# Keys and queries of both attentions turned into scaled fp16 pairs, keys copied to both row halves by DMA

## The chip, the cores and the metric

The kernel runs on one core of a Trainium2 chip. The metric is the device time of one execution in microseconds (us), lower is better. "PE" is TensorE's matmul side and "PEld" its weight load, "DVE" VectorE, "ACT" ScalarE, "POOL" GpSimd, and "SP" SyncE, whose queue issues most of the DMAs.

## The reference

Two layers of a diffusion trunk over 512 latent tokens (an 8 x 64 grid) and 256 context tokens, width 1024. Each layer has two attentions side by side, both with 8 query heads of 64 channels, and with normalised keys and queries:

```python
hx = _rmsnorm(x, norm_g) * (1.0 + scale_x) + shift_x
px = hx @ w_in
a_k, a_v, b_k, b_v, a_q, b_q, a_z, b_z, g_a, g_b = _split(px, SPLIT_SIZES)
...
qa = _rmsnorm(hs(a_q, NA_HEADS), q_norm_a)
ka = _rmsnorm(hs(a_k, NA_HEADS), k_norm_a)
a_att = _na_latent(qa, ka, va, cka, cva, rpb, rows)    # 8 x 16 window + bias, all context keys
qb = _rope_2d(_rmsnorm(hs(b_q, GQA_Q_HEADS), q_norm_b), pos_row, pos_col)
kb = _rope_2d(_rmsnorm(hs(b_k, GQA_KV_HEADS), k_norm_b), pos_row, pos_col)
b_att = _gqa_latent(qb, k_all, v_all)                  # 2 key/value heads, all 768 keys
out_x = _merge(a_att, b_att, a_z, b_z, g_a, g_b, w_o_a, w_o_b, w_out)
x_new = x + gate_x * out_x
```

In the first layer the context tokens go through the same steps (six blocks of 128 tokens as queries), in the second only the latent ones (four). The q and k norms are vectors of 64 per layer; the score is q·k / 8, to which the neighbourhood attention (NA below) adds a learned bias. The other attention is called GQ.

## The kernel before

Everything is held to fp32 accuracy with products of two-part numbers. A projection splits its weights into hi and lo (`load_w` L397, `load_w2` L412: a DMA into `raw`, the hi cast on ACT, the subtraction on POOL or DVE) and its activations likewise (`hx`), and `mm3` L433 takes three fp32r matmuls per 128 x 128 piece: lines L435, L436 and L437, which make up most of PE's time. `raw` has three buffers, the pair `whi`/`wlo` eight, so a weight load is issued when a cast has freed a buffer.

A layer runs: projection of NA keys (AK), of NA values (AV), of NA queries (AQ), the NA stage head by head, the GQ projections, the GQ stage head by head, and the output projections. The eight weight tiles of a projection are used by all token blocks; in layer 1 the blocks of AV are worked side by side in separate PSUM tiles. Work of the gates and of the z projections (`fill`, matmuls of L435 to L437 into `psf` and `psx`) is spread between the heads' scores, so that PE has something to do while DVE and ACT work on a softmax.

After a projection of keys or queries, each block of 128 tokens is normalised by head (`evac_na` L547, `rope_heads` L578) into a tile `y` (`rr` for GQ) with tokens on the rows. `turn` L524 brings it to channels on the rows: four PE transposes into a PSUM tile, then one ACT operation into the fp32 tile `ka`, `qa`, `kb` or `qb` (L545 with the norm's gain, L543 without). A 128-row piece of it has two heads, one in each half of the rows. `hp["lag"]` says how many blocks a turn runs behind its projection. At the start of a head the pair for the scores is made:

- `stage_k` L869: a DVE cast of 64 x 768 (L872), an ACT cast to the other half of the rows (L873), a DVE subtraction (L874; on POOL for GQ, with a further ACT copy L876).
- `stage_q` L878: an ACT cast (L883) and a DVE subtraction into the other half (L884). `qs` then has q's hi part in one half and its lo part in the other, and a matmul over all 128 rows against `kh`, which has the key in both halves, adds up both products.
- the scores are two fp32r matmuls for each piece, with `kh` and with `kl`: L890 and L891 for GQ and the context, L978 for the NA windows.

Behind the scores come, for NA, one DVE operation that negates the scores, adds the bias and takes the minimum (L981), an exp on ACT (L984), and a normalisation; for GQ, L1161 and L1162 in the same roles, and for the context's own queries L903, L905 and L909. The probabilities become an fp16 pair `h` (L841 on ACT, L842 on POOL or DVE) that SP's DMA transposes (L846) into `ht`, from which the value matmuls (L1002 to L1012, L1178, L1179) read. A head's bias comes by three DMAs (`load_bias` L952) into `bint` and `bedg`. Heads are pipelined: the scores of a head are issued before the values of the head ahead of it.

The program is scheduled: a list scheduler with its own timeline puts the instructions of each engine into an order, so code that is written early can land later. `behind` L473 holds a piece to program order on one engine. On each engine, SP's queue included, instructions run in that order, each waiting for its semaphores.

## Time and profile before

| | |
|---|---|
| median of three runs | 1108.3 us |
| lowest, highest | 1107.35, 1112.0 us |
| the profiled execution | 1111.07 us, span 1109.3 us |
| granted clock of TensorE, mean | 0.991 |
| DVE, ACT, POOL busy | 69%, 56%, 43% of the span |
| DMA, mean | 155 GB/s |

A view by windows gives, for a stretch of the span, the busy time of each engine in it, so a window's width less PE's busy time is PE's idle time there. A view by groups gives for each line and tile how many instructions there were, their summed time, the mean of one in ns, and behind the second bar the idle time just ahead of them with what ended it. In a timeline the columns are start, duration, engine, line and operands; matmuls overlap, so their cadence is read from the starts.

### The profile page before, as it was taken

The page shows a single profiled execution, that of the slowest core. Times are in us where ns is not written, and L with a number is a line of the kernel's source. Part 1 is how long each engine was busy: PE and PEld are TensorE (multiplying, and loading weights), DVE is VectorE, ACT ScalarE, POOL GpSimd, SP SyncE. Part 2 cuts the span into 40 slices and gives each one's busy share as a digit, 9 for nine tenths or more (in the row PEclk, how much of TensorE's full clock was granted, in tenths as well). Part 3 has the DMA queues.
Part 4 walks back from the last instruction along what each step waited for, and adds up shares of the span by engine and source line. Part 5 has one row for each costly group of instructions (what it writes and reads, how often), then busy time and mean ns, then how long its engine had stood idle before and what let it go on. Part 6 is the DMA issues. An engine that isn't in the chain of part 4 may idle for free. (4 is left out here: it accounts for less than half of the span.)

```text
span 1109.3 us, 16937 instructions
## 1 busy us (share of the span) xinstructions
PE 1075.5 (97%) x5672; PEld 879.1 (79%) x5672; DVE 767.4 (69%) x1600; ACT 617.1 (56%) x1236; POOL 473.1 (43%) x397
## 2 busy tenths in 40 slices
PE   8999999999999989989999999999999999999998
PEld 5688888788888868767788878888877888777677
DVE  4667889975377487766777785366997665677473
ACT  6454279776433566765330275444899446786430
POOL 1054235555257154463621354232355472564531
PEclk9999999999999999998999999999999999999999
DMA  9455324554543379789633542453565536879642
GB/s 370 146 171 153 90 68 111 128 138 120 169 131 127 100 184 215 166 228 228 213 101 124 157 147 78 140 163 101 134 149 130 156 107 171 199 229 239 188 152 77
DMA packets 236000, 171.79 MB, mean 155 GB/s; under 512 B 160140, under 2 KB 201864, under 8 KB 234248
## 3 DMA queue, kind: packets, MB, share of 16 engines
q1 hardware_dynamic: 228576, 156.31, 51.6%
q0 software_dynamic: 2368, 7.87, 2.1%
q10 hardware_dynamic: 4968, 6.53, 1.8%
q8 instruction: 45, 0.74, 0.3%
q14 instruction: 43, 0.35, 0.1%
HBM read 115.58 MB, written 17.32 MB: 120 GB/s over the span
## 5 line engine op out<-in xcount | busy, mean ns | idle before, releaser
L842 POOL TENSOR_TENSOR h<-p,h 128x256 f16<-128x256 f32 (+2 forms) x104 | 113.6, 1101 | 160.0 <-ACT h L841 117.7
L422 POOL TENSOR_TENSOR wlo<-raw,whi 128x512 fp32r<-128x512 f32 x70 | 98.0, 1406 | 131.6 <-ACT whi L420 98.7
L435 PE MATMUL psf<-hx,whi 128*128 128x512 f32 (+1 forms) x360 | 138.2, 384 | 2.2 <-DVE zt L627 1.2
L436 PE MATMUL psf<-hx,whi 128*128 128x512 f32 (+1 forms) x360 | 136.1, 378 | 0.0
L437 PE MATMUL psf<-hx,wlo 128*128 128x512 f32 (+1 forms) x360 | 136.1, 378 | 0.0
L435 PE MATMUL psx<-whi,hx 128*128 128x512 f32 (+1 forms) x328 | 121.0, 372 | 0.0
L437 PE MATMUL psx<-whi,hx 128*128 128x512 f32 (+1 forms) x328 | 120.0, 367 | 0.0
L420 ACT CAST whi<-raw 128x512 fp32r<-128x512 f32 x136 | 83.2, 620 | 65.5 <-DMA raw<-in_w_in_dram 46.9
L436 PE MATMUL psx<-wlo,hx 128*128 128x512 f32 (+1 forms) x328 | 119.6, 366 | 0.0
L408 POOL TENSOR_TENSOR wlo<-raw,whi 128x512 fp32r<-128x512 f32 x40 | 59.8, 1499 | 117.7 <-ACT whi L405 74.6
L405 ACT CAST whi<-raw 128x512 fp32r<-128x512 f32 x88 | 54.3, 623 | 96.7 <-PE psx L437 34.2
L508 POOL TENSOR_TENSOR ss<-ss,ehalf 128x8 f32<-128x8 f32 (+2 forms) x40 | 63.6, 1593 | 77.2 <-DVE ss L505 72.2
L841 ACT CAST h<-p 128x256 f16<-128x256 f32 (+2 forms) x136 | 81.7, 616 | 5.3 <-DMA ht<-h 1.3
L422 DVE TENSOR_TENSOR wlo<-raw,whi 128x512 fp32r<-128x512 f32 x66 | 65.3, 992 | 25.9 <-ACT whi L420 24.3
L1161 DVE CUSTOM_DVE_ANT_0 p<-pss,vb 128x768 f32<-128x768 f32 x64 | 60.2, 953 | 31.0 <-PE pss L891 28.9
L1162 ACT ACTIVATE p<-pss,mx 128x768 f32<-128x768 f32 x64 | 57.6, 901 | 41.1 <-DVE mx L1161 40.4
L435 PEld LDWEIGHTS psf<-hx,whi 128*128 128x128 f32 x360 | 68.3, 190 | 14.9 <-ACT zt L625 1.9
L437 PEld LDWEIGHTS psf<-hx,wlo 128*128 128x128 f32 x360 | 68.2, 190 | 12.0
L436 PEld LDWEIGHTS psf<-hx,whi 128*128 128x128 f32 x360 | 68.3, 190 | 10.9
L437 PEld LDWEIGHTS psx<-whi,hx 128*128 128x128 f32 x328 | 61.9, 189 | 10.2
L436 PEld LDWEIGHTS psx<-wlo,hx 128*128 128x128 f32 x328 | 62.0, 189 | 9.5
L435 PEld LDWEIGHTS psx<-whi,hx 128*128 128x128 f32 x328 | 61.8, 189 | 9.1 <-issue 0.2
(338 smaller groups left out, 2984.7 us busy)
## 6 DMA issues: line engine op xcount, KB each, us to landing
raw<-in_w_in_dram SPq DMA_DIRECT2D x168, 256.0 KB, 3.0
rawb<-in_w_ada_dram SPq DMA_DIRECT2D x48, 256.0 KB, 2.8
raw<-in_w_out_dram SPq DMA_DIRECT2D x32, 256.0 KB, 2.9
tg<-gs SPq DMA_DIRECT2D x4, 1536.0 KB, 9.9
rawx<-in_w_ada_dram SPq DMA_DIRECT2D x4, 1024.0 KB, 10.3
rawy<-in_w_ada_dram SPq DMA_DIRECT2D x4, 1024.0 KB, 10.3
gs<-zt ACTq DMA_DIRECT2D x16, 256.0 KB, 2.6
raw<-in_w_o_a_dram SPq DMA_DIRECT2D x16, 256.0 KB, 3.1
```

Of the source, the lines that this page charges most:

```text
L405: S.copy(hi[:, :n], raw[:, :n])
L408: e.tensor_tensor(lo[:, :n], raw[:, :n], F(hi[:, :n]), ALU.subtract)
L420: S.copy(hi, raw)
L422: lo_eng(i).tensor_tensor(lo, raw, F(hi), ALU.subtract)
L435: T.matmul(ps, lhs[0], rhs[0], start=first, stop=False)
L436: T.matmul(ps, lhs[0], rhs[1], start=False, stop=False)
L437: T.matmul(ps, lhs[1], rhs[0], start=False, stop=last)
L508: G.tensor_tensor(ss, ss, ehalf[:, :n], ALU.pow)
L841: S.copy(h[:, 0], p[:, :n])
L842: eng.tensor_tensor(h[:, 1], p[:, :n], h[:, 0], ALU.subtract)
L1161: V.tensor_tensor_reduce(p, pss, lift, -1.0, 3e38, ALU.add, ALU.min, mx[:, 0:1])
L1162: S.activation(p, pss, AF.Exp, bias=mx[:, 0:1], accum_out=r[:, i:i + 1])
```

## The change

`turn` no longer writes fp32. It writes an fp16 pair: hi on ACT, lo as (scaled) source minus hi on DVE, both from the PSUM tile. For keys hi and lo are two tiles of all 128 rows. For queries it works by half of the rows: a head's hi goes to its own half and its lo to the other, so that one 128-row slice is what `qs` was. The blocks 0 and 3 of NA queries, whose tokens are placed in two pieces, take two such sets at half width. `stage_q` and its tiles go; a head uses a slice. `stage_k` becomes two SP DMAs of 64 x 2 x 768 from SBUF to SBUF for an NA head, and two per key head (64 x 1536) for GQ. All score matmuls are fp16.

So that fp16 holds the numbers, the gains are scaled up by 2048 over their largest entry (`head_scales`, `na_scales` and the GQ preparation: a few small DVE operations and a DMA of the norms on ACT's queue), and the scores are scaled back where they are read: a factor in L981, L1161 and the exps. The NA bias has to be scaled the other way: in each layer's AV projection the whole table (1 MB and 0.5 MB) is loaded into `za`, scaled by three ACT operations, and stored to two DRAM tiles, from which `load_bias` reads.

```diff
+    def head_scales(rows, inv, up):
+        S.activation(rows, rows, AF.Abs)
+        V.tensor_reduce(inv, rows, AX, ALU.max)
+        V.tensor_scalar(inv, inv, G_MIN, 1.0 / H_UP, ALU.max, ALU.mult)
+        V.reciprocal(up, inv)
+    def na_scales():
+        t = stp.tile([128, 2, 2, 2], F32, name="nscale")
+        inv, up = t[:, 0], t[:, 1]
+        flat = lambda a: a.rearrange("p l i -> p (l i)")
+        head_scales(nrow, flat(inv), flat(up))
+        V.tensor_tensor(gcol[:, 48:52], gcol[:, 48:52], flat(up), ALU.mult)
+        V.tensor_tensor(na_dq, inv[:, :, 0], inv[:, :, 1], ALU.mult)
+        V.tensor_scalar(na_ndq, na_dq, -1.0, None, ALU.mult)
+        V.tensor_tensor(na_up, up[:, :, 0], up[:, :, 1], ALU.mult)
...
-            src = pt.rearrange("p (j s n) -> p j s n", j=npair, s=2)
-            d = dst[:, :, 0:512].rearrange("p j (s n) -> p j s n", n=64)
-            if t == 0:
-                d = d[:, :, 0:3:2, :]
+            cuts = [(0, 64, 0), (64, 128, 128)] if t == 0 else [(0, 64, 448), (64, 128, 64)]
+        else:
+            cuts = [(0, 128, 128 * t + (64 if perm and t < 4 else 0))]
+        def pair(hi, lo, x, g):
+            if g is None:
+                S.copy(hi, x)
+                V.tensor_tensor(lo, x, hi, ALU.subtract)
             else:
-                src, d = src[:, :, ::-1, :], d[:, :, 1:8:6, :]
-        else:
-            c0 = 128 * t + (64 if perm and t < 4 else 0)
-            src = pt.rearrange("p (j n) -> p j n", j=npair)
-            d = dst[:, :, c0:c0 + 128]
-        if g is None:
-            S.copy(d, src)
-        else:
-            S.activation(d, src, AF.Copy, scale=g)
+                S.activation(hi, x, AF.Copy, scale=g)
+                V.scalar_tensor_tensor(lo, x, g, hi, ALU.mult, ALU.subtract)
+        kind, a, b = dst
+        for n0, n1, c0 in cuts:
+            x = pt.rearrange("p (j n) -> p j n", j=npair)[:, :, n0:n1]
+            da, db = [d[:, :, c0:c0 + n1 - n0] for d in (a, b)]
+            if kind == "k":
+                pair(da, db, x, g)
+                continue
+            for e, d in enumerate((da, db)):
+                own, other = slice(64 * e, 64 * e + 64), slice(64 - 64 * e, 128 - 64 * e)
+                pair(d[own], d[other], x[own], None if g is None else g[own])
...
+        za = big("za")
+        ti, te = za[:, 0:2048].rearrange("p (h n) -> p h n", h=8), za[:, 2048:3072].rearrange("p (h n) -> p h n", h=8)
+        nc.sync.dma_start(ti, bias_int[l].rearrange("h p n -> p h n"))
+        nc.sync.dma_start(te, bias_edge[l].rearrange("h p n -> p h n"))
+        def scale_bias():
+            for c in range(3):
+                c0 = 1024 * c
+                S.activation(za[:, c0:c0 + 1024], za[:, c0:c0 + 1024], AF.Copy, scale=na_up[:, l:l + 1])
+            nc.sync.dma_start(b_int[l].rearrange("h p n -> p h n"), ti)
+            nc.sync.dma_start(b_edge[l].rearrange("h p n -> p h n"), te)
         for t in range(6):
             tok_proj(w, 512, a_hx, t, evac_va)
+            if t == 3:
+                behind(ON_ACT, scale_bias)
             if first:
...
-            def k_tile(e, zero):
-                kh = att["p"].tile([128, 768], F32R, tag=f"kh{e}", name=nm("kh"), bufs=1)
-                kl = att["p"].tile([128, 768], F32R, tag=f"kl{e}", name=nm("kl"), bufs=1)
-                if zero:
-                    V.tensor_scalar(rows(kl, 1 - e).rearrange("p (a b) -> p a b", b=128),
-                                    rows(ident, 1 - e).unsqueeze(1).to_broadcast([64, 6, 128]),
-                                    0.0, None, ALU.mult)
-                return kh, kl
-            def stage_k(src, e, kh, kl, dup):
-                k = rows(src, e)
-                V.tensor_copy(rows(kh, e), k)
-                S.copy(rows(kh, 1 - e), k)
-                (G if dup else V).tensor_tensor(rows(kl, e), k, F(rows(kh, e)), ALU.subtract)
-                if dup:
-                    S.copy(rows(kl, 1 - e), F(rows(kl, e)))
-            def stage_q(src, e):
-                n = 768 if first else 512
-                qs = att["p"].tile([128, n], F32R, tag=f"qs{e}", name=nm("qs"), bufs=1)
-                q = rows(src, e)[:, :n]
-                S.copy(rows(qs, e), q)
-                V.tensor_tensor(rows(qs, 1 - e), q, F(rows(qs, e)), ALU.subtract)
-                return qs
+            def stage_k(src, j, e, to):
+                for half in range(2):
+                    nc.sync.dma_start(rows(to, half), rows(src, e)[:, :, j, :])
+            def q_pair(src, e, j):
+                return src[:, e, j, :]
...
-                if late:
-                    V.tensor_scalar(mx, mx, P_LOG, None, ALU.add)
+                dq = gq_dq if late else na_dq[:, l:l + 1]
+                V.tensor_scalar(mx, mx, dq, P_LOG if late else 0.0, ALU.mult, ALU.add)
                 p = p_tile()
                 r = sp.tile([128, 2], F32, tag="r", name=nm("r"), bufs=8)
                 for i in range(2):
                     S.activation(p[:, 256 * i:256 * i + 256], pss[:, 256 * i:256 * i + 256], AF.Exp,
-                                 bias=mx[:, i:i + 1], accum_out=r[:, i:i + 1])
+                                 bias=mx[:, i:i + 1], scale=dq, accum_out=r[:, i:i + 1])
                 if not late:
                     softmax_tail(p, 512, r, mx, [(0, 256), (256, 512)])
...
-                nc.sync.dma_start(bint[:, 0:256], bias_int[l, h])
+                nc.sync.dma_start(bint[:, 0:256], b_int[l][h])
                 for i in range(2):
                     nc.sync.dma_start(bedg[64 * i:64 * i + 64, 128 * i:128 * i + 128],
-                                        bias_edge[l, h, 64 * i:64 * i + 64])
+                                        b_edge[l][h, 64 * i:64 * i + 64])
             turns = big("ht").bitcast(F16)
...
+                    V.tensor_tensor_reduce(p[:, :512], pss, bedg if i == 0 else bint, na_ndq[:, l:l + 1], 3e38,
                                            ALU.add, ALU.min, mx[:, 0:1])
                     r = sp.tile([128, 2], F32, tag="r", name=nm("r"), bufs=8)
...
-            akt = [k_tile(e, True) for e in range(2)]
+            akt = [att["p"].tile([128, 2, 768], F16, name=nm("kk"), bufs=1) for _ in range(2)]
             def na_first(h):
                 j, e = h // 2, h % 2
-                kh, kl = akt[e]
-                stage_k(kav[:, j, :], e, kh, kl, False)
-                q = stage_q(qav[:, j, :], e)
+                kh, kl = akt[e][:, 0], akt[e][:, 1]
+                stage_k(kav, j, e, akt[e])
+                q = q_pair(qav, e, j)
                 st = na_scores(h, q, kh, kl)
                 if not first:
...
-            V.tensor_scalar(gbc[:, 1, :], gbc[:, 1, :], 8.0, None, ALU.mult)
+            vbig = big("vb")
+            g_inv, g_up = vbig[:, 2952:2954], vbig[:, 2954:2956]
+            gq_dq, gq_ndq = vbig[:, 2956:2957], vbig[:, 2957:2958]
+            g_abs = vbig[:, 1920:2048].rearrange("p (a d) -> p a d", a=2)
+            S.copy(g_abs, gbc)
+            head_scales(g_abs, g_inv, g_up)
+            V.tensor_scalar(gbc[:, 0, :], gbc[:, 0, :], g_up[:, 0:1], None, ALU.mult)
+            V.tensor_scalar(gbc[:, 1, :], gbc[:, 1, :], g_up[:, 1:2], 8.0, ALU.mult, ALU.mult)
+            V.tensor_tensor(gq_dq, g_inv[:, 0:1], g_inv[:, 1:2], ALU.mult)
+            V.tensor_scalar(gq_ndq, gq_dq, -1.0, None, ALU.mult)
+            V.tensor_scalar(vbig[:, 2950:2951], g_up[:, 0:1], g_up[:, 1:2], -P_LOG, ALU.mult, ALU.mult)
             def make_tabs(i):
...
+            kbv = hp["p"].tile([128, 2, 1, 768], F16, name=nm("kb"), bufs=1)
+            kb_to = ("k", kbv[:, 0], kbv[:, 1])
+            gkt = big("gk").bitcast(F16)[:, 0:3072].rearrange("p (e x n) -> p e x n", e=2, x=2)
             def evac_bkv(t, ps):
                 rs = head_rstd(ps[:, 0:128], 2)
...
-                    stage_k(kbv[:, 0, :], e, gkt[e][0], gkt[e][1], True)
+                    stage_k(kbv, 0, e, gkt[:, e])
...
-                    V.tensor_tensor_reduce(p, pss, lift, -1.0, 3e38, ALU.add, ALU.min, mx[:, 0:1])
-                    S.activation(p, pss, AF.Exp, bias=mx[:, 0:1], accum_out=r[:, i:i + 1])
+                    V.tensor_tensor_reduce(p, pss, lift, gq_ndq, 3e38, ALU.add, ALU.min, mx[:, 0:1])
+                    S.activation(p, pss, AF.Exp, bias=mx[:, 0:1], scale=gq_dq, accum_out=r[:, i:i + 1])
                     turned(p, 768, ht[:, i], G if i in SPLIT_POOL else V)
```

Three places in the engines' queues. First SP at the AV projection of layer 1; `raw` are tiles of AV's weights, `cb` and `rawb` belong to the modulation. Before:

```order
L403 DMA raw_7300<-in_w_in_dram 128x512
L286 DMA cb_7282<-cd 128x512
L290 DMA rawb_7448<-in_w_ada_dram 128x512
L290 DMA rawb_7451<-in_w_ada_dram 128x512
L403 DMA raw_7306<-in_w_in_dram 128x512
L403 DMA raw_7312<-in_w_in_dram 128x512
L403 DMA raw_7318<-in_w_in_dram 128x512
```

and with the change:

```order
L428 DMA raw_7334<-in_w_in_dram 128x512
L311 DMA cb_7316<-cd 128x512
L315 DMA rawb_7490<-in_w_ada_dram 128x512
L315 DMA rawb_7493<-in_w_ada_dram 128x512
L428 DMA raw_7340<-in_w_in_dram 128x512
L798 DMA za_7370<-in_bias_int_dram 128x8x256
L799 DMA za_7370<-in_bias_edge_dram 128x8x128
L428 DMA raw_7346<-in_w_in_dram 128x512
```

The two loads of the bias table stand between the fourth (`raw_7340`) and the fifth (`raw_7346`) of AV's eight weight tiles.

Second, PE with the change, where the fifth of these tiles is first used (`whi_7348` is the cast of `raw_7346`; `whi_7324`, `whi_7330`, `whi_7336` are of the first three; `psx_7373`, `psx_7401`, `psf_7429`, `psx_7457` are four token blocks of AV). The first matmul of AV is 44 rows ahead of the row with `whi_7348`:

```order
L462 MATMUL psx_7457<-whi_7324,hx_6712 128x512
L460 MATMUL psx_7457<-whi_7330,hx_6710 128x512
L461 MATMUL psx_7457<-wlo_7332,hx_6710 128x512
L462 MATMUL psx_7457<-whi_7330,hx_6712 128x512
L460 MATMUL psx_7373<-whi_7348,hx_6711 128x512
L460 MATMUL psx_7401<-whi_7348,hx_6711 128x512
```

The four blocks run side by side through the first four weight tiles; before, a block was mostly finished ahead of the next.

Third, SP in the NA stage of layer 1, for about one head. Before:

```order
L846 DMA_TRANSPOSE ht_1571_7883<-h_1581_7912 128x4x64 x2
L846 DMA_TRANSPOSE ht_1571_7883<-h_1586_7928 128x4x128
L846 DMA_TRANSPOSE ht_1571_7883<-h_1591_7943 128x4x128
L953 DMA bint_1569_7877<-in_bias_int_dram 128x256
L955 DMA bedg_1570_7878<-in_bias_edge_dram 64x128 x2
L629 DMA zs_79<-zt_1708_8460 128x512
L846 DMA_TRANSPOSE ht_1571_7883<-h_1596_7958 128x4x128
```

and with the change:

```order
L910 DMA kk_1554_7947<-ka_1373_7046 64x2x768 x2
L893 DMA_TRANSPOSE ht_1553_7946<-h_1560_7967 128x4x64 x2
L893 DMA_TRANSPOSE ht_1553_7946<-h_1565_7983 128x4x128
L893 DMA_TRANSPOSE ht_1553_7946<-h_1570_7998 128x4x128
L893 DMA_TRANSPOSE ht_1553_7946<-h_1575_8013 128x4x128
L981 DMA bint_1551_7940<-b_int1_84 128x256
```

The copies of a coming head's keys (`kk`) stand ahead of the transposes of the present head. They wait until PE has issued the last score that reads the same `kk` tile, two heads back.

More of the change, by code (lines that the diff above doesn't have):

```diff
@@ L35 @@
 P_UP = 2.0 ** 14
+H_UP = 2.0 ** 11
+G_MIN = 1.0e-6
 SPLIT_POOL = (1, 3)
@@ L130, in hybrid_kernel @@
     cd = drp.tile([16, 128], F32, name="cd")
+    b_int = [drp.tile([8, 128, 256], F32, name=f"b_int{i}") for i in range(2)]
+    b_edge = [drp.tile([8, 128, 128], F32, name=f"b_edge{i}") for i in range(2)]
     gs = [drp.tile([128, 4, NTOK], F32, name=f"gs{c}") for c in range(4)]
@@ L779, in layer @@
         for t in range(qt):
-            tok_proj(w, 512, a_hx, t, evac_na(qav, True, gq, YB if first else 4))
+            tok_proj(w, 512, a_hx, t, evac_na(("q", qav[:, 0], qav[:, 1]), True, gq, YB if first else 4))
             if t == 0:
@@ L980, in na_scores @@
                     mx = sp.tile([128, 2], F32, tag="mx", name=nm("mx"), bufs=8)
-                    V.tensor_tensor_reduce(p[:, :512], pss, bedg if i == 0 else bint, -1.0, 3e38,
+                    V.tensor_tensor_reduce(p[:, :512], pss, bedg if i == 0 else bint, na_ndq[:, l:l + 1], 3e38,
                                            ALU.add, ALU.min, mx[:, 0:1])
@@ L1479, in _layout @@
                                 + [d['b_ada'][:, 2048:].reshape(16, 128)])
-    d['gvec'] = np.concatenate([d[n][l] for l in range(2) for n in ('q_norm_b', 'k_norm_b')])[None]
+    d['gvec'] = np.concatenate([d[n + b][l] for b in 'ba' for l in range(2) for n in ('q_norm_', 'k_norm_')])[None]
     qc, qr = np.arange(128) // 8, np.arange(128) % 8
```

37 lines of the change are left out of this document (19 added, 18 removed).

## The prediction

> **What bounds the kernel now.** I read the page's busy times first, then PE's idle time by windows, then what PE waited for.
>
> ```profile
> PE 1075.5 (97%) x5672; PEld 879.1 (79%) x5672; DVE 767.4 (69%) x1600; ACT 617.1 (56%) x1236; POOL 473.1 (43%) x397
> 92.00:145.00 53.00, 53.00 (x262) 43.73 (x261) 42.20 (x98) 20.31 (x33) 17.45 (x10) 1.00 0.39 113
> 145.00:250.00 105.00, 101.69 (x616) 86.86 (x615) 94.47 (x250) 86.14 (x193) 52.41 (x56) 1.00 0.48 117
> 380.00:460.00 80.00, 73.59 (x409) 60.33 (x408) 61.60 (x111) 52.59 (x103) 38.17 (x26) 0.96 0.77 181
> 460.00:530.00 70.00, 65.13 (x355) 51.91 (x353) 45.34 (x82) 44.99 (x85) 35.90 (x26) 0.95 0.88 224
> 782.40:862.10 79.70, 78.08 (x416) 62.01 (x416) 70.91 (x197) 72.44 (x160) 40.58 (x45) 1.00 0.59 138
> 410.00:420.00 10.00, 8.47 (x27) 6.67 (x28) 8.85 (x19) 5.50 (x12) 3.70 (x4) 0.66 0.70 165
> 500.00:510.00 10.00, 9.78 (x44) 8.84 (x45) 4.38 (x11) 5.62 (x11) 4.57 (x4) 0.68 1.16 245
> ```
>
> The columns are the window, its width, busy times of PE, PEld, DVE, ACT and POOL with counts, the granted clock, the DMA share and GB/s. PE is busy 1075.5 of 1109.3 us, so 33.8 us are idle in all. Work taken from DVE or ACT is worth at most what it takes out of these 33.8 us; work taken from PE counts nearly in full. A third of the idle time, 6.41 + 4.87 = 11.3 us, lies in the GQ stage of layer 0 (380 to 530). There the clock also fell twice: 8.47 x 0.34 = 2.9 us and 9.78 x 0.32 = 3.1 us of PE time were lost to it. So 17.3 us are lost in that stage. In the NA stages (145 to 250, and 782 to 862 in layer 1) PE idles 3.3 and 1.6 us. In 92 to 145, where keys and queries of layer 0 are projected, it never idles.
>
> ```profile
> PE pss L890 <- ACT p L1162: 4.3, 3, 2.7
> PE pst L853 <- DVE mx L905: 2.9, 1, 2.9
> 406.77 4.61 DVE L297 CUSTOM_DVE_ANT_0 rawb<-rawb,vb 128x512 f32<-128x512 f32 x1
> 493.94 3.60 DVE L842 TENSOR_TENSOR h<-p,h 128x768 f16<-128x768 f32 x1 [0.32 <-ACT h L841]
> 489.54 7.18 POOL L672 TENSOR_TENSOR gal<-za,gah 128x768 fp32r<-128x768 f32 x4
> ```
>
> These are PE's two largest waits and what lies behind them. The DVE operations at 406.77 and 493.94 were held for 4.61 and 3.60 us. The second ends, at 497.5, just after POOL's four back-to-back operations (489.54 + 7.18 = 496.7). L905 and L1162 of the waits stood behind them. The change removes neither of these DVE operations.
>
> **PE's own gain.** Score matmuls go from fp32r to fp16. Their counts, one of each pair:
>
> ```profile
> L890 PE MATMUL pss<-gk,qs 128*128 128x512 f32 x64 | 28.5, 445 | 5.6 <-ACT p L1162 4.3 <-ACT p L909 1.3
> L890 PE MATMUL pss<-gk,qs 128*128 128x256 f32 x80 | 23.1, 292 | 0.0
> L978 PE MATMUL pss<-kh,qs 128*128 128x512 f32 x48 | 19.2, 400 | 0.0
> L890 PE MATMUL pss<-kh,qs 128*128 128x384 f32 x16 | 6.3, 391 | 0.0
> 938.23 0.39 PE L890 MATMUL pss<-gk,qs 128*128 128x512 f32 x1
> 938.46 0.40 PE L891 MATMUL pss<-gk,qs 128*128 128x512 f32 x1
> 938.70 0.28 PE L890 MATMUL pss<-gk,qs 128*128 128x256 f32 x1
> 946.96 0.38 PE L1179 MATMUL pst<-ht,vb 128*128 128x512 f16 x1
> 947.18 0.38 PE L1178 MATMUL pst<-ht,vb 128*128 128x512 f16 x1
> 947.39 0.38 PE L1179 MATMUL pst<-ht,vb 128*128 128x512 f16 x1
> ```
>
> Twice 64 x 512, 80 x 256, 48 x 512 and 16 x 384, with 16 x 128 and 16 x 256 beside the latter in NA, are 180,224 columns, or 352 times 512. The fp32r starts are (938.70 - 938.23) / 2 = 0.235 us apart, the fp16 starts (947.39 - 946.96) / 2 = 0.215. That is 352 x 0.019 = 6.6 us; I take **-6.4**, since pieces of 128 columns can hardly gain. The other end is 0, if the weight loads of short pieces stood in the way.
>
> ```profile
> L891 PEld LDWEIGHTS pss<-gk,qs 128*128 128x128 f32 x144 | 28.0, 194 | 4.3
> L1178 PEld LDWEIGHTS <-vb 128*128 128x128 f16 x96 | 9.4, 98 | 12.1 <-issue 2.6 <-DMA raw<-in_w_o_a_dram 0.3
> ```
>
> But the load shrinks from 194 to 98 ns, below the 108 ns of a 256-column piece, so I stay near -6.4.
>
> **Work moved on DVE and ACT.**
>
> ```profile
> L872 DVE CAST kh<-ka 64x768 fp32r<-64x768 f32 x16 | 10.0, 625 | 2.3 <-PE pst L529 1.4 <-PE pss L978 0.7
> L874 DVE TENSOR_TENSOR kl<-ka,kh 64x768 fp32r<-64x768 f32 x16 | 16.6, 1038 | 0.3
> L884 DVE TENSOR_TENSOR qs<-qb,qs 64x768 fp32r<-64x768 f32 x8 | 9.3, 1159 | 2.4 <-ACT qs L883 2.2
> L884 DVE TENSOR_TENSOR qs<-qa,qs 64x768 fp32r<-64x768 f32 x8 | 8.8, 1099 | 0.2
> L873 ACT CAST kh<-ka 64x768 fp32r<-64x768 f32 x16 | 13.3, 833 | 1.3 <-PE pss L890 0.7 <-PE pss L978 0.3
> L832 DVE SCALAR_TENSOR_TENSOR ho<-psv,vsa,ho 64x512 f32<-64x512 f32 x14 | 10.5, 749 | 12.4 <-ACT ho L831 11.6 <-POOL h L842 0.7
> L545 ACT ACTIVATE qa<-pst,gcol 128x512 f32<-128x512 f32 x10 | 6.7, 684 | 3.6 <-PE pst L529 3.6
> ```
>
> An NA head of layer 0 loses 0.63 + 1.04 + 1.10 = 2.8 us on DVE and 0.83 on ACT, and its q cast besides. A GQ head there loses 1.16 us on DVE. Added is, at the turns, one DVE operation like L832's (a product and a difference out of PSUM) for each block of keys and two for each of queries, 0.75 us each, and a second ACT operation of 0.68 for queries. For the six query blocks of layer 0 these are 9.0 us on DVE. They fall into 92 to 145, where DVE has 42.2 of 53: it then has about 51, still covered by PE's full 53 us, and the first heads' staging no longer follows. Should DVE be late there, the transposes of `y` are late next, by up to the 9.0 us less the 2.8 us of each of the first two heads, 3.4. I take **+1** (0 to +4).
>
> In the NA stages DVE and ACT have less to do by 3 us a head; PE idles there 4.9 us in all. I take **-2** (0 to -4.9). In the GQ stage of layer 0 the relief is 8 x 1.16 = 9.3 of DVE's 107 us, a twelfth, and about as much of ACT's. Since the held operations remain but the order around them is new, I take somewhat under a third of the 17.3: **-5** (0 to -17.3; a new collision as long as the old ones would be +6: a wait of 2.9 and 3.1 of clock).
>
> The small operations of the scales, the norm's DMA and one more DVE operation for each context score lie beside PE's full stretches: **+0.5** (0 to +2; a start-up stall has no other work to hide it).
>
> **The bias table ahead of AV's weights in layer 1.** 1.5 MB are loaded by SP right ahead of the fifth weight tile.
>
> ```profile
> tg<-gs SPq DMA_DIRECT2D x4, 1536.0 KB, 9.9
> DMA to landing us min/median/max: 10.2/10.2/10.2
> 686.60 19.04 SPq L403 DMA_DIRECT2D raw<-in_w_in_dram  x13
> 686.41 0.62 ACT L405 CAST whi<-raw 128x512 fp32r<-128x512 f32 x1
> 690.04 0.62 PE L435 MATMUL psx<-whi,hx 128*128 128x512 f32 x2
> ```
>
> A load of this size took 9.9 us, and a 256 KB weight tile issued right behind such loads, at 489.20, landed after 10.2 us (the second row, that tile alone). The fourth weight tile of AV is issued at 686.60, the table at about 687.1 and 687.6, the fifth tile at 688.1; it lands at 698.3, and with a cast of 0.62 and a subtraction of 1.5 it is ready at 700.4. PE begins AV at about 690.3, and the new order puts 43 matmuls of 0.23 us and a set of transposes (0.6) ahead of the first use: 700.8. That is met by 0.4 us; **+1** (0 to +8: a landing 5 us later, and 3 us at the low clock). The stores and the table of layer 0 have over ten microseconds to spare on both sides of their places.
>
> [...]
>
> **The key copies on SP.**
>
> ```profile
> L846 SPq DMA_TRANSPOSE ht<-h x40: 1169/1218/1981, 782.4 to 860.8; - x40
> L953 SPq DMA_DIRECT2D bint<-in_bias_int_dram x16: 340/532/1134, 136.1 to 844.4; - x16
> L955 SPq DMA_DIRECT2D bedg<-in_bias_edge_dram x32: 472/550/993, 138.1 to 840.3; - x32
> ```
>
> Forty transposes in 78.4 us are eight heads of 10.0 us in layer 1. Of these SP spends 5 x 1.22 + 0.53 + 2 x 0.55 = 7.7 us on the head itself and some 1.5 us on weights and stores that it issues in between: 9.2 of 10.0. Two copies of the kind of L955 (64 rows) add 1.1: 10.3. So SP becomes as full as PE in this stage. A head's order may still shift load into the neighbouring stretches, which is why I take **+2.5** and not 8 x 0.3 with queueing on top (0 to +11, below). In layer 0 a head has more blocks and SP has room. The GQ copies have tens of microseconds until the first score.
>
> **Sum:** -6.4 + 1 - 2 - 5 + 0.5 + 1 + 2.5 = -8.4. The profiled execution took 1111.07, 2.8 above the median of the three runs; from its own time the sum gives 1102.7, from the median 1099.9. Later times stand beside the median, so I forecast **1100**.
>
> **Rivals.** (A) The two collisions and low clocks in the GQ stage vanish altogether: -17.3 in place of -5 and -4.9 in place of -2, so 1085 at best, and 1092 with half of that. For it speaks that DVE and ACT are both lighter, against it that L297, L842 and L672 stay. Chance 0.13.
>
> (B) The gain is returned: fp16 scores only make PE wait for the softmax, which is no shorter, or the weight loads take the 6.4 back. Then what remains is -7 + 1 + 0.5 + 1 + 2.5 = -2, **1106**. For it speaks that L890 waited for ACT's exp; against it that most stretches have no idle time at all. Chance 0.20.
>
> (C) SP becomes the bound of the NA stage in layer 1. If each head waits 1 us more in the queue (a transpose blocked behind a copy that waits for PE's last score of two heads back), a head takes 11.4 and not 10.0: 8 x 1.4 = 11 in place of 2.5, and the gains of the NA and GQ stages are not there: -6.4 + 1 + 0.5 + 1 + 11 = +7, **1115**. What is queued behind a copy is the transposes, for which PE's values wait, and behind these the next scores. It decides from the point where SP's work for a head passes PE's. For it speaks the 9.2 of 10.0; against it that a copy's turn comes once the scores it waits for are issued. Chance 0.22.
>
> **Numbers.** The forecast has 0.45. A measurement of this kernel tells about 0.5%, 5.5 us, from no change: faster is below 1102.8, slower above 1113.8. The forecast's own range, from the neighbouring values of its terms, is 1093 to 1107; 1102.8 cuts it at two thirds, so 0.32 of it is faster and 0.13 the same. A is all faster. Of B 0.03 is faster, 0.15 the same and 0.02 slower, of C 0.02 the same and 0.20 slower. That gives 0.48, 0.30 and 0.22. The losing ends of several terms (+4, +8, +6) can come together and go beyond C, so 0.05 moves from the same to slower. The range of 8 in 10 runs from 1089 (between A's half and its best) to 1118, a little beyond C.
>
> **What would show it.** Score starts 0.215 us apart, and PE's busy time down by about 6 us; L872 to L884 gone and DVE busy by some 20 us less; the first fifth-tile matmul of AV in layer 1 waiting for at most 1 us; PE's waits for `ht` in the NA stage of layer 1 below 3 us. Wrong would be a longer cadence with the separate weight loads, PE idle above 6 us in that NA stage with SP's queue without a gap, or new waits for DVE in 92 to 145.

## The result and the profile after

The changed kernel takes 1138.95 us (median of 5 runs, 1136.84 to 1141.91) against 1109.04 for the kernel before (5 runs): a ratio of 1.027, 95% interval 1.024 to 1.030. It is 30 us slower where 8 us less were forecast. Sixteen further versions were run to find out which part of the change costs what; the fastest of them stands at 0.997 of the kernel before.

The busy times on the page of the changed kernel's profiled execution (span 1140.0 us):

```profile
PE 1080.4 (95%) x5672; PEld 849.9 (75%) x5672; DVE 756.2 (66%) x1627; ACT 608.6 (53%) x1219; POOL 451.1 (40%) x393
```

PE's idle time goes from 33.8 to 1140.0 - 1080.4 = 59.6 us. DVE and ACT both have less to do, by 11 and 9 us, so the change did lighten them, but the time is longer all the same. PE's busy time rises by 5 us although its score matmuls are shorter (381 ns for 512 columns in NA, where they took 397 to 400); more of it runs at the low clock (mean granted clock 0.983 against 0.991).

To see where the time went, both programs are cut at the same events: the first and last score of each NA stage, the first DVE scan of each GQ stage, its last value matmul. The widths, read from the starts of these instructions:

| stage (us) | before | after | difference |
|---|---|---|---|
| start to first NA score, layer 0 | 151.5 | 156.2 | +4.7 |
| NA stage of layer 0 | 115.8 | 114.5 | -1.3 |
| GQ projections of layer 0 | 109.4 | 109.9 | +0.5 |
| GQ stage of layer 0 | 161.3 | 161.2 | -0.1 |
| to the first NA score of layer 1 | 238.2 | 244.7 | +6.5 |
| NA stage and GQ projections of layer 1 | 148.5 | 165.1 | +16.6 |
| GQ stage of layer 1 | 119.6 | 121.0 | +1.4 |
| rest | 65.0 | 67.4 | +2.4 |

The NA stage of layer 1 and the projections behind it are taken together, since the schedule moves `fill` matmuls between them. Windows of both, before first, then after (width, busy times of PE, PEld, DVE, ACT, POOL with counts, clock, DMA share, GB/s):

```profile
776.20:924.70 148.50, 146.31 (x799) 120.46 (x799) 115.47 (x284) 106.54 (x231) 77.35 (x75) 1.00 0.52 136
```

```profile
786.50:951.60 165.10, 149.02 (x798) 115.23 (x796) 108.87 (x281) 97.94 (x218) 72.22 (x73) 0.98 0.53 137
```

The same number of matmuls, 799 and 798, takes 16.6 us longer: PE idles 16.1 us in place of 2.2, and the clock drops to 0.98. DVE, ACT and POOL have less to do, and the DMA engines move 137 GB/s against 136. SP's queue is not in these rows. Its timeline in the changed kernel, and PE's behind it:

```profile
847.04 1.13 SPq L983 DMA_DIRECT2D bedg<-b_edge  x2
848.27 14.02 SPq L893 DMA_TRANSPOSE ht<-h  x10
862.34 0.57 SPq L662 DMA_DIRECT2D gs<-zt  x1
863.01 0.94 SPq L442 DMA_DIRECT2D raw<-in_w_in_dram  x2
864.04 1.20 SPq L893 DMA_TRANSPOSE ht<-h  x1
```

```profile
866.93 0.79 PE L460 MATMUL psx<-hx,whi 128*128 128x512 f32 x1 [6.15 <-ACT whi L445]
867.52 0.63 PE L461 MATMUL psx<-hx,whi 128*128 128x512 f32 x1
867.95 0.63 PE L460 MATMUL psf<-hx,whi 128*128 128x512 f32 x1
868.38 0.63 PE L461 MATMUL psf<-hx,whi 128*128 128x512 f32 x1
```

Ten transposes in a row keep SP for 14 us; the weight tiles for PE's filling work stand behind them and are issued at 863.0, cast at 866.3, and PE has waited 6.15 us. After that its starts are 0.43 us apart and not 0.23, at a granted clock of 0.50 from 866.9 to 872.0. The wait is named after ACT's cast (L445), but ACT itself had sat idle for 1.03 us until the DMA of that tile landed, and the DMA had its turn in the queue only at 863.0.

PE's largest waits over the whole run show the other losers:

```profile
PE psf L460 <- DVE tg L740: 9.0, 6, 3.6
PE psx L460 <- ACT whi L445: 6.6, 2, 6.1
PE pss L918 <- ACT p L1199: 6.5, 3, 3.5
PE psv L1030 <- DVE ho L879: 3.7, 2, 2.3
```

`L1199` is the exp of GQ and `tg` a DVE operation of the output gates that shares DVE with GQ's scans. Two rows of the groups show what became of the operations in these chains:

```profile
L1198 DVE CUSTOM_DVE_ANT_0 p<-pss,vb 128x768 f32<-128x768 f32 x64 | 64.1, 1013 | 28.7 <-PE pss L919 23.9 <-POOL h L889 4.3
L1199 ACT ACTIVATE p<-pss,mx,vb 128x768 f32<-128x768 f32 x64 | 63.5, 993 | 46.8 <-DVE mx L1198 44.2 <-PE psv L900 2.4
```

and the same of the kernel before, with the exp of the context's scores:

```profile
L1161 DVE CUSTOM_DVE_ANT_0 p<-pss,vb 128x768 f32<-128x768 f32 x64 | 60.2, 953 | 31.0 <-PE pss L891 28.9 <-POOL h L842 1.5
L1162 ACT ACTIVATE p<-pss,mx 128x768 f32<-128x768 f32 x64 | 57.6, 901 | 41.1 <-DVE mx L1161 40.4 <-ACT zt L625 0.4
L909 ACT ACTIVATE p<-pss,mx 128x256 f32<-128x256 f32 x32 | 14.9, 469 | 10.3 <-DVE mx L905 6.4 <-DVE h L842 3.6 <-DVE mx L903 0.2
```

The scan took 953 ns and the exp 901; now 1013 and 993. The shape is the same; what is new is that the factor is read from memory (`vb` among the exp's inputs) where it was a constant of the instruction.

### The profile page after: what moved, and what is told of

Same layout as the page of the kernel before. It is cut to its first block, busy times and chain, and to the rows that moved or that the text cites. A ratio compares the mean times of both kernels' runs of the same rounds, so it can differ in the third digit from the quotient of the medians.

```text
span 1140.0 us, 16941 instructions
## 1 busy us (share of the span) xinstructions
PE 1080.4 (95%) x5672; PEld 849.9 (75%) x5672; DVE 756.2 (66%) x1627; ACT 608.6 (53%) x1219; POOL 451.1 (40%) x393
## 5 line engine op out<-in xcount | busy, mean ns | idle before, releaser
L889 POOL TENSOR_TENSOR h<-p,h 128x256 f16<-128x256 f32 (+2 forms) x104 | 108.5, 1051 | 166.0 <-ACT h L888 127.9
L460 PE MATMUL psf<-hx,whi 128*128 128x512 f32 (+1 forms) x360 | 140.6, 391 | 4.4 <-ACT zt L658 2.2
L461 PE MATMUL psf<-hx,whi 128*128 128x512 f32 (+1 forms) x360 | 137.7, 383 | 0.0
L445 ACT CAST whi<-raw 128x512 fp32r<-128x512 f32 x136 | 83.1, 621 | 79.2 <-DMA raw<-in_w_in_dram 48.7
L460 PE MATMUL psx<-whi,hx 128*128 128x512 f32 (+1 forms) x328 | 121.0, 371 | 0.0
L447 DVE TENSOR_TENSOR wlo<-raw,whi 128x512 fp32r<-128x512 f32 x66 | 70.0, 1063 | 42.2 <-ACT whi L445 41.0
L1199 ACT ACTIVATE p<-pss,mx,vb 128x768 f32<-128x768 f32 x64 | 63.5, 993 | 46.8 <-DVE mx L1198 44.2
L1198 DVE CUSTOM_DVE_ANT_0 p<-pss,vb 128x768 f32<-128x768 f32 x64 | 64.1, 1013 | 28.7 <-PE pss L919 23.9
L460 PE MATMUL psx<-hx,whi 128*128 128x256 f32 (+1 forms) x208 | 70.5, 339 | 6.6 <-ACT whi L445 6.6
L462 PE MATMUL psx<-hx,wlo 128*128 128x256 f32 (+1 forms) x208 | 69.8, 335 | 0.2 <-POOL wlo L447 0.2
## 6 DMA issues: line engine op xcount, KB each, us to landing
rawy<-in_w_ada_dram SPq DMA_DIRECT2D x4, 1024.0 KB, 11.1
```

Source lines behind the costliest of these rows:

```text
L445: S.copy(hi, raw)
L447: lo_eng(i).tensor_tensor(lo, raw, F(hi), ALU.subtract)
L460: T.matmul(ps, lhs[0], rhs[0], start=first, stop=False)
L461: T.matmul(ps, lhs[0], rhs[1], start=False, stop=False)
L462: T.matmul(ps, lhs[1], rhs[0], start=False, stop=last)
L889: eng.tensor_tensor(h[:, 1], p[:, :n], h[:, 0], ALU.subtract)
```

## The experiments

Two kinds of runs. The first take one part out of the changed kernel; the second put one part alone into the kernel before. All are compared with runs of the kernel before on the same chip (1108.6 to 1109.3). Each edit goes through the scheduler again, so the order of other instructions can change with it.

### Parts taken out of the change

**Key copies of NA from ACT's queue** (in `stage_k`; `late` is true for NA heads):

```diff
-                    nc.sync.dma_start(rows(to, half), rows(src, e)[:, :, j, :])
+                    (S if late else nc.sync).dma_start(rows(to, half), rows(src, e)[:, :, j, :])
```

> The key copies of the NA heads are issued by ACT's queue instead of SP's; nothing else differs from the changed kernel (1139 us). Theory Q (SP's queue is full in the NA stage of layer 1, and weight tiles and transposes wait behind its other work): the stage and the GQ projections behind it, 165 us from first score to first GQ score in the changed kernel against 148.5 before, shrink to 150 to 155, and the time to 1122 to 1130. Theory D (it is the DMA traffic or the landing of the copies themselves that costs): within 3 us of 1139. Theory S (the softmax chains are longer, because exp and the DVE scan take their factor from memory): within 3 us of 1139 too.

1131.8 us (ratio 1.021, 1.020 to 1.023): 7 us are gone, and the stage and projections of layer 1 take 159.3 us, not the expected 150 to 155. So SP's queue matters. What the rest is, the copies themselves or their waits in ACT's order, this run does not tell.

**Key copies by engines** (the DMAs stay for GQ):

```diff
+                if late:
+                    V.tensor_copy(rows(to, e), rows(src, e)[:, :, j, :])
+                    S.copy(rows(to, 1 - e), rows(src, e)[:, :, j, :])
+                    return
                 for half in range(2):
                     nc.sync.dma_start(rows(to, half), rows(src, e)[:, :, j, :])
```

> The NA keys are put into both halves by one DVE copy and one ACT copy of 64 x 2 x 768 fp16 for each head, with no DMA. Theory Q: as with ACT's queue or better, 1120 to 1130, less what the copies cost on engines that are about 70% busy there. Theory D: the same gain, since the traffic goes too, so this run beats the one with ACT's queue by more than 5 us only if D holds. Theory S: within 4 us of 1139.

1122.7 us (1.013, 1.011 to 1.016), 16 us below the changed kernel; the two stages take 151.7. It beats the run from ACT's queue by 9 us, which by what was expected speaks for the copies' traffic as well. In the kernel before, the runs below rule the traffic out; from ACT's queue the copies cost 2.9 us there, and what the other 6 us of this difference are stays open.

**No bias table:** the loads, the scaling and the stores go, and the heads read the unscaled table, so the scaling of the NA bias is left out.

> The bias table is neither loaded into za, scaled nor stored; the heads read the unscaled table, so the scaling of the NA bias is left out. Theory Q: the AV stage of layer 1 showed no wait of PE for weights, and the table's loads and stores lie elsewhere in SP's queue than the NA stage, so 1134 to 1140. Rival B (the table's 6 MB of transfers and six ACT operations hold up the start of both layers, 3.3 and 2.9 us, and what follows): 1128 to 1134.

1129.6 us (1.019, 1.017 to 1.021), 9 us less. The start is 2.3 us shorter, the NA stage of layer 0 by 4.5, and the two stages of layer 1 by 6.4.

**Constant factors** in the exps, scans and context maxima (one constant for all; the true scales are left out):

```diff
-                    V.tensor_tensor_reduce(p, pss, lift, gq_ndq, 3e38, ALU.add, ALU.min, mx[:, 0:1])
-                    S.activation(p, pss, AF.Exp, bias=mx[:, 0:1], scale=gq_dq, accum_out=r[:, i:i + 1])
+                    V.tensor_tensor_reduce(p, pss, lift, -2.0e-5, 3e38, ALU.add, ALU.min, mx[:, 0:1])
+                    S.activation(p, pss, AF.Exp, bias=mx[:, 0:1], scale=2.0e-5, accum_out=r[:, i:i + 1])
```

> The factors in the exps, the DVE scans and the context maxima are constants of the program (2.0e-5 for all), not values read from memory; the true scales are left out. Theory S: DVE's L1198 falls from 1013 to about 955 ns and ACT's exp from 993 to about 900 ns, the GQ stages (161.2 and 121.0 us) shrink by 3 to 5 us each, and the time goes to 1128 to 1134. Theory Q: the durations may fall but the time stays within 4 us of 1139, since PE waits in the NA stage of layer 1 for other things.

1128.1 us (1.018, 1.016 to 1.019). The exp is back at 900 ns and the scan at 953 (means), and the GQ stage of layer 0 shrinks from 161.2 to 149.7, with 13 matmuls fewer in it and a granted clock of 1.00 against 0.95; that of layer 1 does not shrink (123.9, with 10 more matmuls in it).

With 16 us for the copies, these gains come to 36 us, more than the loss of 30. Each run is also a new schedule, and two runs that take several parts out at once show that the gains do not add.

**No scales at all** (plain values in the fp16 pairs; neither table nor factors nor the operations for them), key copies on SP:

> The changed kernel with no scaling anywhere: no factors from memory, no bias table through za, no small operations for the scales; the fp16 pairs hold the plain values. Key copies stay on SP. If the three costs add up (table -9.5 by the run without it, constant factors -11 by the run with constants, both from 1139), 1116 to 1122, with the key copies' 8 to 16 us left in the NA stage of layer 1 (at least 160 us from its first score to the first GQ score, 148.5 before). If the order of the schedule decides and not these costs, anything between 1110 and 1135, with the gain in other stages than those of the two single runs (start -2.3, GQ stage of layer 0 -11.5).

1133.3 us (1.022, 1.019 to 1.025): above the expected 1116 to 1122. The start (152.6) and the GQ stage of layer 0 (150.6) have their gains, but the two stages of layer 1 take 164.1 us, as in the changed kernel. So the gain of the table and the factors did not reach these two stages; the next run shows that the copies on SP stand in its way.

**No scales, key copies by engines:**

> The same with the NA keys put into both halves by one DVE and one ACT copy for each head. Theory Q (SP's queue costs the rest): 8 to 16 us below the run before, 1102 to 1110, that is, about the kernel before the change or under it; the NA stage of layer 1 and the GQ projections take 146 to 152 us. If Q was the only cause and the scales only an order's luck, it is the same as the run with engine copies and scales, 1120 to 1125.

1112.7 us (1.004, 1.003 to 1.006), above the expected 1102 to 1110. Now the two stages take 149.6. Copies on SP or on engines are worth 20.7 us here.

### Parts put into the kernel before

**The copies alone.** Two SP DMAs of the changed kernel's bytes for each NA head, into a tile that nobody reads:

```diff
                 stage_k(kav[:, j, :], e, kh, kl, False)
+                for half in range(2):
+                    nc.sync.dma_start(dum[64 * half:64 * half + 64, :], F(kh)[64 * e:64 * e + 64, :])
```

> The kernel before the change, with two more SP copies of 64 x 768 fp32 (192 KB, the bytes of the changed kernel's copies) from SBUF to SBUF for each NA head, into a tile that nobody reads. Theory Q: SP is busy 9.2 of 10.0 us for a head of layer 1, and these take it over that: the NA stage of layer 1 and the GQ projections go from 148.5 to 155 us or more, the time to 1114 to 1126; layer 0, where SP has room, stays within 2 us. Rival T (the copies only hurt because the new kernel's turns and heads are ordered otherwise): 1106 to 1112.

1125.5 us (1.015, 1.012 to 1.018): +16.7 from 32 DMAs that the kernel does not need. The two stages of layer 1:

```profile
773.10:937.70 164.60, 151.56 (x799) 121.32 (x799) 119.40 (x285) 107.48 (x231) 80.20 (x75) 0.98 0.52 137
```

164.6 us for 799 matmuls, where the kernel before took 148.5; the NA stage of layer 0 is unchanged (115.6). PE idles 13.0 us there in place of 2.2 and is busy 5.3 us longer, at a granted clock of 0.98. That the width falls within half a microsecond of the changed kernel's 165.1 is in part luck, since PE's waits are others: the longest is 3.8 us ahead of a value matmul (`psv`, L1002), where the changed kernel's 6.15 us stood ahead of the filling work.

**The same DMAs with next to no bytes,** 64 x 16 in place of 64 x 768 (`dum[..., 0:16]`):

> The kernel before with two more SP copies for each NA head, as in the run with full copies (1125.5 us, stage and GQ projections of layer 1 164.6 instead of 148.5), but of 64 x 16 fp32, 4 KB. Theory Q (what costs is SP's issue time and the waits in its order): 1118 to 1126, the two stages 158 us or more. Theory D (it is the 384 KB a head that the DMA engines carry beside transposes and weights): 1107 to 1113.

1124.7 us (1.014, 1.012 to 1.016), and in the two stages:

```profile
773.90:938.20 164.30, 151.28 (x800) 120.90 (x800) 120.58 (x285) 107.49 (x231) 79.08 (x75) 0.98 0.45 123
```

A fiftieth of the bytes, 4 KB for 192, and the loss is the same. Traffic is ruled out: what costs is that SP issues two more DMAs a head. Their issue times on SP's queue (minimum, median and maximum in ns), with the full bytes, in this run, and of the changed kernel's copies:

```profile
L1044 SPq DMA_DIRECT2D dum<-kh x32: 461/498/1296, 147.4 to 847.8; - x32
```

```profile
L1044 SPq DMA_DIRECT2D dum<-kh x32: 461/500/1032, 146.5 to 848.2; - x32
```

```profile
L910 SPq DMA_DIRECT2D kk<-ka x32: 607/644/1689, 144.7 to 866.6; - x32
```

A rival would be that a copy holds the queue while it waits for its own data or its tile. The traces speak against it. In the changed kernel, between the first and the last transpose of layer 1's NA heads, no pause of SP over 0.11 us stands ahead of a copy; with the full dummy copies there is none over 0.05 from 815 to 850, and with the tiny ones no wait of 0.8 us or more ahead of a copy from 776 to 870. Why two short issues a head are too many is seen in SP's timeline of the kernel before. These five rows have its two longest pauses, 0.69 us ahead of 813.35 and 1.44 ahead of 815.13:

```profile
811.67 0.51 SPq L629 DMA_DIRECT2D zs<-zt  x1
812.29 0.37 SPq L417 DMA_DIRECT2D raw<-in_w_in_dram  x1
813.35 0.34 SPq L953 DMA_DIRECT2D bint<-in_bias_int_dram  x1
815.13 1.16 SPq L955 DMA_DIRECT2D bedg<-in_bias_edge_dram  x2
816.51 7.02 SPq L846 DMA_TRANSPOSE ht<-h  x5
```

From 782.4 to 862.0, the 79.6 us in which the forty transposes are issued, all pauses over 0.3 us come to about 3 us. Otherwise one issue follows the other within 0.3 us, mostly 0.05 to 0.1, and this step between two issues takes queue time too. So the queue had about 0.4 us a head to spare. Two issues of 0.50 us with their steps are about 1.2 us a head, 0.8 more than was free: some 6 us for eight heads, an estimate. PE's longer busy time at the low clock (5.3 us with the full copies) comes on top; the remaining 5 us or so are not split.

**The full copies from ACT's queue:**

```diff
-                    nc.sync.dma_start(dum[64 * half:64 * half + 64, :], F(kh)[64 * e:64 * e + 64, :])
+                    S.dma_start(dum[64 * half:64 * half + 64, :], F(kh)[64 * e:64 * e + 64, :])
```

> The kernel before with the full copies of 192 KB, issued by ACT's queue instead of SP's. Theory Q: most of the 17 us goes, 1108 to 1114; what is left is ACT's issue time. Theory D: 1120 to 1127, as from SP.

1112.2 us (1.003, 1.001 to 1.004), the two stages 153.4. So most of the 16.7 us belongs to SP's queue and not to the copies.

**The factors alone,** 1.0 and -1.0 read from memory:

```diff
-                    S.activation(p, pss, AF.Exp, bias=mx[:, 0:1], accum_out=r[:, i:i + 1])
+                    S.activation(p, pss, AF.Exp, bias=mx[:, 0:1], scale=na_dq[:, l:l + 1], accum_out=r[:, i:i + 1])
```

> The kernel before with the factors of the exps, of the DVE scans and of the context maxima read from memory (1.0 and -1.0), so its results do not change. Theory S: DVE's scan goes from 955 to about 1013 ns, ACT's exp from 902 to about 993, and the time to 1112 to 1120, the excess in the two GQ stages. If S is wrong and the runs with constants owe their gain to another order: 1107 to 1111.

1118.9 us (1.008, 1.005 to 1.011), +9.7. The groups of this run:

```profile
L1163 DVE CUSTOM_DVE_ANT_0 p<-pss,vb,ehalf 128x768 f32<-128x768 f32 x64 | 64.4, 1013 | 30.5 <-PE pss L894 28.2 <-POOL h L845 1.4 <-issue 0.4
L1164 ACT ACTIVATE p<-pss,mx,ehalf 128x768 f32<-128x768 f32 x64 | 63.4, 991 | 49.1 <-DVE mx L1163 48.8
L911 ACT ACTIVATE p<-pss,mx,ehalf 128x256 f32<-128x256 f32 x32 | 17.8, 560 | 14.1 <-DVE mx L907 9.3 <-DVE h L845 3.3 <-DVE r L798 1.3
```

+60 ns for a scan and +90 for an exp, at both lengths of the exp: the context's, of 256 columns, goes from 469 to 560. The stages of GQ are wider by 1.4 and 5.6 us, the two stages of layer 1 by 2.5; the new schedule moved `fill` matmuls between stages, so the excess can't be split more finely.

**The table alone,** with a factor of 1.0:

> The kernel before with the round trip of the bias table (loads into za, three ACT operations with a factor of 1.0, stores, heads read the copy). Theory B (the table costs by itself, up to the 9.5 us by which the run without it was faster): 1112 to 1118, of which some 2 us before the first score of layer 0. Rival: it is covered, 1107 to 1111.

1110.8 us (1.001, 1.000 to 1.003): +1.6, covered. So most of the 9 us that its removal gave belonged to the new schedule or to the state of SP's queue, not to the table's transfers; which of the two, no run tells.

**fp16 score operands alone,** same staging operations as before:

```diff
-                kh = att["p"].tile([128, 768], F32R, tag=f"kh{e}", name=nm("kh"), bufs=1)
+                kh = att["p"].tile([128, 768], F16, tag=f"kh{e}", name=nm("kh"), bufs=1)
```

and so for `kl`, `qs` and `gk`.

> The kernel before the change, with only the type of the scores' operands changed: kh, kl and qs are fp16 tiles, filled by the same ACT, DVE and POOL operations as before. The term of -6.4 us says 1100 to 1104, with PE's score starts 0.215 us apart and PE busy some 6 us less. Rival B (the gain is returned as waits or lost to weight loads): 1106 to 1110.

1106.2 us (0.9985, 0.997 to 1.000). Page and timeline of this run:

```profile
PE 1068.6 (97%) x5672; PEld 844.4 (76%) x5672; DVE 759.2 (69%) x1600; ACT 615.5 (56%) x1236; POOL 472.1 (43%) x397
...
935.50 0.39 PE L890 MATMUL pss<-gk,qs 128*128 128x512 f16 x1
935.72 0.38 PE L891 MATMUL pss<-gk,qs 128*128 128x512 f16 x1
935.94 0.27 PE L890 MATMUL pss<-gk,qs 128*128 128x256 f16 x1
936.05 0.27 PE L891 MATMUL pss<-gk,qs 128*128 128x256 f16 x1
```

PE's busy time falls by 6.9 us and the starts are 0.22 and 0.11 us apart, as reckoned. But only 2.6 us reach the end. PE idles 2.1 us more in the GQ stage of layer 0, 2.0 more in that of layer 1, and 2.6 in the two stages of layer 1.

### Relief for SP

The last four runs move the three bias DMAs of each NA head from SP to another queue.

```diff
-                nc.sync.dma_start(bint[:, 0:256], b_int[l][h])
+                S.dma_start(bint[:, 0:256], b_int[l][h])
```

In the changed kernel, all else as it is:

> The changed kernel as it is, key copies on SP, but the three bias DMAs of each NA head go to ACT's queue: SP is given back 1.6 us a head for the 1.1 to 1.3 us of the copies. Theory Q: the NA stage of layer 1 and the GQ projections go from 165 to 150 to 156 us, the time from 1139 to 1124 to 1130. If the place of the copies in SP's order and not its load costs: over 1133.

1125.0 us (1.014, 1.012 to 1.016), -14, and the two stages take 152.2. The copies stayed on SP, three other issues a head left it: by this run it is SP's load that costs, not the copies' place in its order.

With fp16 operands alone:

> The kernel before with fp16 score operands (1106.2) and the bias DMAs on ACT's queue. If SP's queue is what returned PE's gain in the NA stage of layer 1 (75.9 us there against 71.9 before, with a wait of 3.0 for ht): 1098 to 1103, that stage under 71 us. If not: 1104 to 1109.

1104.7 us (0.997, 0.996 to 0.998), the fastest of all and 0.3% below the kernel before, though slower than expected; the NA stage takes 74.5 us, not under 71, and with the projections behind it 154.6, with 24 matmuls more than in the run without this relief (151.7).

With pairs at the turns, no scales and copies by engines:

> Pairs at the turns, no scales, key copies by DVE and ACT (1112.7), and the bias DMAs on ACT's queue. Theory Q for the rest: the wait of 4.0 for ht at the end of the NA stage and the low clock behind it go, 1103 to 1108. If the pairs at the turns cost elsewhere: 1110 to 1115.

1106.7 us (0.998, 0.997 to 1.000); the two stages now take 141.5 us with 776 matmuls, where they took 149.6 with 780.

And from POOL's queue:

> The same with the bias DMAs on POOL's queue, where POOL is about half idle in the NA stages but its operations for the probabilities stand behind them. Theory Q: like the run with ACT's queue within 4 us; if POOL's own issue is slow, up to 8 us above it.

1107.7 us (0.999, 0.997 to 1.001), the same within the runs' scatter.

## Why the prediction was wrong

Two terms of the sum failed most: +2.5 for the key copies on SP, which measured +16.7 alone, and +0.5 for the scales' operations, which left out the factors, +9.7 alone.

**SP's queue: the mechanism was named, the price was wrong, and so was the case chosen.** The prediction reckoned 9.2 us of SP's time for a head of 10.0, 10.3 with the copies, and then took +2.5 because "a head's order may still shift load into the neighbouring stretches". The copies alone cost 16.7. The step that failed is the 0.8 us a head that this left as room: it adds up issue times without the step from one issue to the next, and in the trace about 0.4 us were free. A copy also took 0.64 us to issue in the changed kernel (median of 32), not the 0.55 of the row it was priced by. Rival C had the copies at +11 with a chance of 0.22 and gave 1115, still too low, and its picture of a copy that waits in the queue for PE's score is not what the trace shows. What it left out: weight tiles stand in the same queue, and in the changed kernel PE's filling work, its cover, ran dry (6.15 us at 860.8), with the clock at 0.50 behind it. The reckoned 10.3 of 10.0 pointed to C more than to the forecast. The prediction's own sign of being wrong, PE idle above 6 us in that NA stage, came: 11.1 us (94.4 wide, 83.3 busy). The issues are not small for the kernel: 32 issues of 0.50 us, of 4 KB each, cost 15.5 us on SP's queue, and the full copies from ACT's queue cost 2.9.

**The factors were not priced.** "The small operations of the scales ... +0.5" counted the operations that the change adds, and not what it does to those that exist: the diff gives 64 GQ exps, 32 context exps and 128 scans a factor from memory. Alone that is +9.7. The direct price of those in GQ, 64 x 0.09 us of exp and 64 x 0.06 of scan, is 9.6 us on ACT and DVE in stages where PE waits for just these; that it comes near the +9.7 is in part chance, since the GQ stages grew by 7.0 and other stages by the rest. An exp took 90 to 92 ns more in the runs (901 to 991 and 993, 469 to 560).

**PE's own gain** of 6.4 was right as PE time (6.9 measured; the rows give 352 x 0.020 = 7.0, where the prediction has 6.6) and wrong as time: 2.6 arrives. That is rival B's mechanism at 0.6 of its size. The 0.2 that the prediction took off for pieces of 128 columns stood on no row; with fp16 operands alone those matmuls took 227 and 219 ns (`kh` and `kl`), where they had taken 237 and 275. The sentence that "work taken from PE counts nearly in full", because PE is 97% busy, is the step that failed here: 6.7 us of new idle time of PE stand in the three stretches named above, 4.5 over the whole run. Which waits took them is open. SP's queue alone it is not, since with the bias off SP 4.2 us arrive (1108.9 to 1104.7), of which the relief itself may be a part.

**The relief of DVE and ACT,** -2 and -5, brought nothing in the changed kernel: PE idles 3.1 us in the NA stage of layer 0 as before (3.3), and 15.5 in the GQ stage of layer 0 against 11.9. DVE's total fell by 11 us and not 20; the factors returned 64 x 0.06 us twice, for GQ and NA, 7.7 in all. In the second of these stages the held operations came back at other places, as feared; one of them is a DVE operation on 128 x 2 elements that took 3.39 us:

```profile
529.05 3.39 DVE L933 TENSOR_SCALAR mx<-mx,vb 128x2 f32<-128x2 f32 x1
```

The factors hid a part of this gain: in three runs with the pairs and without such factors (the constants, and no scales with the copies on SP or on engines), that stage runs at a granted clock of 0.99 to 1.00, not 0.95, and takes 149.3 to 150.6 us. Some of that is matmuls that moved to other stages (798 against 811), and PE's idle time there, 11.6 us with constant factors, is still near that of the kernel before.

**The bias table ahead of AV's weights** was put at +1. The fifth weight tile landed 8.5 us after its issue, near the 10.2 taken, and PE did not wait for weights between 690 and 730: 0 at that place, +1.6 for the whole table alone.

**The projections of layer 0:** +1 for DVE. DVE was busy 51.3 of 58 us there (92 to 150), near the reckoned 51, and PE waited once, 2.2 us for DVE (L660), ahead of the first score.

**What adds up:** the parts put into the kernel before give +16.7 (copies), +9.7 (factors), +1.6 (table) and -2.6 (fp16 operands), 25.4 of 29.9 us. Since the gains in the changed kernel did not add, this sum is no proof of the shares. The pairs at the turns are the part that was not run alone. Without scales and with the copies by engines they stand 6.5 us above fp16 operands alone, and 2.0 above once both have the bias off SP; how the rest splits between them and the schedule is open.

## What to carry to other kernels

Count the time of the queue that issues DMAs as that of an engine: its operations for a period, each with its own issue time and the step to the next one, against the period, and everything that stands behind them in order. Here the issue times were reckoned at 92% of a head, and with the steps between them some 4% of the time was free in the trace; two more short DMAs a head cost 15.5 us at 4 KB each and 16.7 at 192 KB. Three others a head moved to ACT's queue gave 14 us back in the changed kernel. When a constant becomes a value that is read from memory, price it in each instruction that uses it (here 90 ns an exp and 60 a scan), above all in a chain that the busiest engine waits for.

## What was not expected of the hardware

An exp with its factor from memory takes 90 ns more at 256 and at 768 columns alike (469 to 560, 901 to 991), and a DVE scan 60 ns more (953 to 1013). SP's dummy copies of 4 KB and of 192 KB cost the queue the same, 0.50 us each (medians 500 and 498 ns); the changed kernel's copies, also 192 KB but of two pieces a row, took 0.64. A transpose costs it 1.2. A single wait of PE of 6.15 us was followed by 5 us of matmuls at 0.43 us instead of 0.23, at a granted clock of 0.50.
